# A tile of their own for the extra tokens' values, and a second room for the last chunk's probabilities

## The chip, the cores and the metric

The kernel runs on one core of one Trainium2 chip. Time is the device time of one execution in microseconds (us). The kernel before took 1063.71 us (median of 3 runs, 1061.87 to 1066.89). One further execution was profiled; it took 1059.23 us.

## What is computed

One layer of a hybrid decoder. A prompt of 2048 tokens (16 chunks of 128) and 48 extra tokens (8 sequences of 4 decode tokens, and 16 meta tokens) are layer-normed and projected by one input matrix. Half of the width goes through an mLSTM, evaluated chunk by chunk with a carried state; the other half through sliding-window attention (window 128, meta tokens visible to all, one learned sink per head). Both are gated, projected and merged with the residual:

```python
def mlstm_chunk(state, q, k, v, log_i, log_f):
    ...
    qk = jnp.einsum('bthd,bshd->btsh', q, k) * w
    num = jnp.einsum('btsh,bshd->bthd', qk, v) + jnp.einsum('bthk,bhkv->bthv', q, c) * s_inter[..., None]
    ...
    c_new = decay[..., None, None] * c + jnp.einsum('bsh,bshk,bshv->bhkv', w_state, k, v)
...
    s = jnp.einsum('bnqkgd,bnskd->bnkgqs', qb, kcat)
    s = jnp.where(mask[None, :, None, None], s, -jnp.inf)
    o_real = jnp.einsum('bnkgqs,bnskd->bnqkgd', sink_softmax(s, sink), vcat)
...
    mix = jnp.concatenate([y_m, y_a], axis=-1).astype(w_o.dtype) @ w_o
    return layer_norm(DN_ALPHA * x + mix.astype(x.dtype), g, b)
```

## The kernel before

All large products run as three f16 products of split numbers (high and low halves). A projection of one chunk by one 512-wide weight is therefore 24 matmuls of 128x512 (`proj`, lines 296 to 301), summed in one PSUM tile `pj`. There are two such tiles, and a projection can only start when one has been read out by VectorE.

**Phase A** (to about 550 us) takes the 16 chunks through the mLSTM. `a_steps(n)` projects queries, keys, values and output gate (`a_proj(n, 0..3)`, the weights `w_q`, `w_k`, `w_v`, `w_o`), reads each out (L430 for the values, L433 for the others), and does the recurrence: gates (`a_gate`, L513 and L516), running sums (`m_rows`, L749 to L759), weights (`m_weights`, L768 to L787), scores (`m_S`, L803), outputs (`m_num`, L816 and L817), state (`m_kv`, L832). Between these steps `jobs()` is advanced: first the decode tokens' recurrence (`d_prepare`, `d_head`), later the other weights' preparation. Before the loop the extra tokens are projected by the same four weights (`proj_e`, L307 and L308); the results `qe`, `ke`, `ve`, `oe` are written to DRAM as `e_d`, and each `d_head(h)` reads its head from there into `eh` (in the tile `da`), which its first matmul, the transpose L699, needs. `kwe` and `ve` also make the meta tokens' state (L651).

A chunk's values lie in `vaug[n % 2]`, two tiles of 4 heads by 129 columns whose last column is one. The extra tokens' values `ve` are put into `vaug[1]`, which is also the tile of chunk 1.

**Phase B** runs the attention, the gates and the output projection chunk by chunk. `s_unit(n, u)` treats two heads: scores (L1271), masked maximum (L1272), exponentials (L1278), and the split of the probabilities into `hl` (high half by ScalarE, L1279; low half by VectorE, L1280). After every second unit one DMA transpose takes `hl` to `pT`, which `s_pv` (L1324) multiplies with the values. There is one `hl` tile, so unit 2 of a chunk may write it only when the transpose of units 0 and 1 has read it.

Tiles come from pools by tag: a tile of a tag with one buffer can be written when the one before it has been read for the last time. The tag `wkv` has one buffer, which holds in turn the layer-norm rows `gbr`, the arenas of the extra tokens (`e_arena`, 2048 words a partition, handed out piece by piece by `take`) and, in phase B, the key and value weights.

The order of the instructions on each engine is not the order of the code. A scheduler sets it at build time from its own estimate of when each instruction can run. On the chip each engine then goes through its list strictly in order, and an instruction whose input is late holds everything behind it. SyncE (SP) issues all the DMAs, in order as well.

Of the kernel before, what the change touches and what calls it, by code (L numbers as in the profile page):

```python
# [9 lines left out]
F16 = mybir.dt.float16  # L10
# [6 lines left out]
P = 128  # L17
D = 1024
KT = 8
NCH = 16  # L20
NM = 16
NS = 32
NE = NS + NM
H = 4
# [17 lines left out]
def tile_hymba_step(  # L42
# [7 lines left out]
    V, A, G, T, S = nc.vector, nc.scalar, nc.gpsimd, nc.tensor, nc.sync  # L50
# [4 lines left out]
    mn = ctx.enter_context(tc.tile_pool(name="mn", bufs=1))  # L55
# [9 lines left out]
    def pt(shape):  # L65
        return psum("pt", shape, 3)
# [14 lines left out]
    def work(tag, shape, dt=F32, bufs=None):  # L81
        return mn.tile(shape, dt, tag=tag, name=tag, bufs=bufs or KB4.get(tag, 1))
# [23 lines left out]
    def dmat(out, in_):  # L106
        return dma(out, in_, S.dma_start_transpose)
# [108 lines left out]
    vaug = [cst.tile([P, H, 129], F32, name=f"vaug{i}") for i in range(2)]  # L216
# [319 lines left out]
    def e_arena():  # L536
        return Arena(mn.tile([P, 2048], F32, tag="wkv", name="ea"))

    E = St()
    ea = e_arena()  # L540
# [2 lines left out]
    qe = work("qs", [P, 512])[:NE]  # L543
    ke = work("At", [P, 512])[:NE]
    oe = work("g", [P, 512])[:NE]
    ve = vaug[1][:NE]

    sto = stage(512, "w")
    load(sto, w_a[3])
# [9 lines left out]
    hl = work("hl", [P, 2, D], F16)  # L559
    ln0_(xe, NE, hl.rearrange("p c d -> p (c d)").bitcast(BF16)[:NE])  # L560
    split_e(EE[:, 0], xe, NE, s_x)
    dmat(ET, EE[:, 0])
    xef = ea.take(8 * NE).rearrange("p (k t) -> p k t", t=NE)
    ps = pt([P, 8, NE])
    for j in range(8):
        T.transpose(ps[:, j], xe[:, j * P:(j + 1) * P], ident[:NE, :NE])
# [80 lines left out]
    for j in range(2):  # L647
        ps = po([P, 2, 256])
        for i in range(2):
            h = 2 * j + i  # L650
# [605 lines left out]
    def s_unit(n, u):  # L1256

        c = cb[n]
        pvc = cb.get(n - 1)
        lo = 0 if pvc is not None else P  # L1260
        if u % 2 == 0:
            c.hl = work("hl", [P, 2, 4, 256], F16)
        hl, q, h0 = c.hl, u % 2, 2 * u
        mxs, nb, sums = c.mxs, c.nb, c.sums
        mask = swamask[:, c.half, lo:]
        p = work(("g", "SI")[u % 2], [P, 2, NW])
        for i in range(2):
            h = h0 + i
            ps = pt([P, NW])
            for x in range(2):  # L1270
                T.matmul(ps[:, lo:], c.qT[:, h], kTs[:, 2 * (h // 4) + x, lo:], start=(x == 0), stop=(x == 1))  # L1271
            V.tensor_tensor_reduce(p[:, i, lo:], ps[:, lo:], mask, sc_s, sink60[:, h:h + 1],  # L1272
                                   op0=ALU.add, op1=ALU.max, accum_out=mxs[:, h:h + 1])
        hs = slice(h0, h0 + 2)
        V.tensor_scalar(nb[:, hs], mxs[:, hs], -1.0, LN2x12, op0=ALU.mult, op1=ALU.add)  # L1275
        for i in range(2):
            h = h0 + i
            A.activation(p[:, i, lo:], p[:, i, lo:], AF.Exp, bias=nb[:, h:h + 1], accum_out=sums[:, h:h + 1])  # L1278
        A.activation(hl[:, 0, 2 * q:2 * q + 2, lo:], p[:, :, lo:2 * P], AF.Copy)  # L1279
        V.tensor_tensor(hl[:, 1, 2 * q:2 * q + 2, lo:], p[:, :, lo:2 * P], hl[:, 0, 2 * q:2 * q + 2, lo:],  # L1280
                        op=ALU.subtract)
        m = c.mhl[:, u // 2, :, 2 * q:2 * q + 2]
        A.activation(m[:, 0], p[:, :, 2 * P:], AF.Copy)  # L1283
        G.tensor_tensor(m[:, 1], p[:, :, 2 * P:], m[:, 0], op=ALU.subtract)  # L1284
        if lo:
            G.memset(hl[:, :, 2 * q:2 * q + 2, 0:P], 0.0)
        if q:
            pT = work("stg", [P, 2, 4, 2, P], F16)
            dmat(out=pT.rearrange("p c h e q -> p (c h e) q"),
                                  in_=hl.rearrange("p c h k -> p (c h k)"))  # L1290
            c.PT.append(pT)
# [88 lines left out]
    for n in range(NCH - 1):  # L1380
        b_load(n + 1)
        b_q(n)
        b_kv(n)
        if n > 0:
            s_pv(n - 1)
        b_az(n)
        if n == 2:
            b_out(0)
        s_start(n)
        s_unit(n, 0)  # L1390
        s_unit(n, 1)
        b_z(n)
        s_unit(n, 2)
        s_unit(n, 3)
        s_sums(n)
        if n == 0:
            z = work("xs", [P, D])[:NS]
            dma(z, ze_d)
            final(z, NS, y_s)
        elif 1 < n < NCH - 2:  # L1400
            b_out(n - 1)
            cb.pop(n - 2, None)

    n = NCH - 1
# [113 lines left out]
```

## Time and profile before

| | |
|---|---|
| time, median of 3 runs | 1063.71 us (1061.87 to 1066.89) |
| profiled execution | 1059.23 us, of which 1057.4 us are the span from the first to the last instruction |
| TensorE busy with matmuls (PE) | 1026.1 us |
| VectorE (DVE) busy | 728.7 us |
| ScalarE (ACT) busy | 441.3 us |
| GpSimd (POOL) busy | 247.6 us |

In a row of the timeline stand: start in us, length in us, engine, line, operation, output<-inputs by the program's names, output<-input (partitions x elements, type), count. In brackets stands how long the engine was idle just before, and what ended that. In a row of the waits view: the waiting instruction, what it waited for, us in total, times, longest. In a row of the windows view: the stretch and its length, then for each engine the busy time (and the number of instructions), the clock granted to TensorE as a share of full, the busy share of the DMA engines, and GB/s. SPq is SyncE's queue, which issues DMAs.

### The profile page before, as it was taken

How to read it: one execution, taken by the hardware profiler on the slowest of the kernel's cores; microseconds unless marked ns; L12 is line 12 of the kernel's file. 1: busy time of each engine (PE TensorE's matmuls, PEld its weight loads, DVE VectorE, ACT ScalarE, POOL GpSimd, SP SyncE). 2: the span in 40 equal slices, each digit the busy share in tenths (PEclk: the TensorE clock that was granted, in tenths of full speed). 3: DMA queues.
4: the chain of work that ended last, by engine and by line, in shares of the span. 5: the costliest groups of instructions: out<-in, count | busy, mean ns of one | idle time of the engine just before them, and what ended most of it. 6: DMA issues, size and time to landing. Idle time of an engine off the chain costs nothing.

```text
span 1057.4 us, 17650 instructions
## 1 busy us (share of the span) xinstructions
PE 1026.1 (97%) x6399; PEld 571.0 (54%) x6399; DVE 728.7 (69%) x2056; ACT 441.3 (42%) x1112; POOL 247.6 (23%) x270
## 2 busy tenths in 40 slices
PE   7998999999999999999999999999999999999996
PEld 3544666655556555555565555555555455555552
DVE  5996876767766887787557676656566566666674
ACT  5783333336244554552334334343334333343430
POOL 2101313211111001013111332233331233332322
PEclk9998999999999999999999999999999999999998
DMA  9946366464794775755866463555445555545452
GB/s 332 267 133 164 99 145 154 115 187 88 233 236 123 222 247 140 231 133 160 291 188 124 92 160 89 132 131 117 108 113 127 128 124 139 108 102 135 113 114 76
DMA packets 245809, 161.83 MB, mean 153 GB/s; under 512 B 207945, under 2 KB 220953, under 8 KB 244409
## 3 DMA queue, kind: packets, MB, share of 16 engines
q1 hardware_dynamic: 245722, 160.70, 58.3%
q8 instruction: 50, 0.82, 0.3%
q14 instruction: 37, 0.30, 0.1%
HBM read 68.22 MB, written 43.58 MB: 106 GB/s over the span
## 4 chain that ended last, share of the span: by engine, by line
PE 69%; DMA 11%; DVE 10%; ACT 6%; issue 3%; POOL 1%; SPq 1%; DVEq 0%; ACTq 0%
PE pj L1351 14%; PE pj L301 14%; PE pj L298 14%; PE pj L299 14%; DMA stg<-hl 3%; PE pt L1271 3%; PE po L1324 2%; DMA stg<-in_dram 1%; DMA xT<-hl 1%; DMA kT<-kh 1%; ACT w_o L259 1%; DMA wd_o<-w_o 1%; DVE w_o L276 1%; PE po L816 1%; PE po L817 1%
## 5 line engine op out<-in xcount | busy, mean ns | idle before, releaser
L301 PEld LDWEIGHTS <-xT 128*128 128x128 f16 x992 | 96.9, 98 | 98.2 <-issue 1.0
L299 PEld LDWEIGHTS <-xT 128*128 128x128 f16 x992 | 97.4, 98 | 96.7 <-issue 5.2
L298 PEld LDWEIGHTS <-xT 128*128 128x128 f16 x992 | 97.4, 98 | 94.1 <-issue 2.8
L1351 PEld LDWEIGHTS <-EE 128*128 128x128 f16 x720 | 70.3, 98 | 79.0
L1351 PE MATMUL pj<-wr_o,EE 128*128 128x512 f16 x360 | 82.3, 379 | 0.0
L1351 PE MATMUL pj<-w_o,EE 128*128 128x512 f16 x360 | 82.1, 379 | 0.0
L1278 ACT ACTIVATE SI<-SI,nb 128x272 f32<-128x272 f32 (+1 forms) x64 | 32.4, 507 | 66.0 <-DVE nb L1275 66.0
L298 PE MATMUL pj<-w_o,xT 128*128 128x512 f16 x120 | 46.9, 390 | 3.2 <-DVE vaug L430 3.2
L1278 ACT ACTIVATE g<-g,nb 128x272 f32<-128x272 f32 (+1 forms) x64 | 32.2, 503 | 42.4 <-DVE nb L1275 42.4
L1284 POOL TENSOR_TENSOR mhl<-SI,mhl 128x32 f16<-128x32 f32 x32 | 12.6, 395 | 157.6 <-ACT mhl L1283 157.6
L298 PE MATMUL pj<-wr_az,xT 128*128 128x512 f16 x128 | 48.5, 379 | 0.0
L299 PE MATMUL pj<-wr_z,xT 128*128 128x512 f16 x128 | 48.5, 379 | 0.0
L298 PE MATMUL pj<-wr_aq,xT 128*128 128x512 f16 x128 | 48.5, 379 | 0.0
L299 PE MATMUL pj<-wr_aq,xT 128*128 128x512 f16 x128 | 48.5, 379 | 0.0
L299 PE MATMUL pj<-wr_az,xT 128*128 128x512 f16 x128 | 48.5, 379 | 0.0
L298 PE MATMUL pj<-wr_z,xT 128*128 128x512 f16 x128 | 48.5, 379 | 0.0
L793 POOL TENSOR_TENSOR qs<-qs,SI 128x512 f32<-128x512 f32 x16 | 20.9, 1307 | 113.5 <-ACT SI L784 113.3
L299 PE MATMUL pj<-w_o,xT 128*128 128x512 f16 x120 | 46.7, 390 | 0.0
L1181 POOL TENSOR_TENSOR xs<-xs,gb 128x1024 f32<-128x1024 f32 (+1 forms) x16 | 42.8, 2674 | 15.4 <-DMA stg<-hl 9.3
L298 PE MATMUL pj<-w_v,xT 128*128 128x512 f16 x120 | 46.0, 383 | 0.0
L299 PE MATMUL pj<-w_v,xT 128*128 128x512 f16 x120 | 45.8, 382 | 0.0
L792 POOL TENSOR_TENSOR qs<-qT 128x512 f32<-128x512 f16 x16 | 20.2, 1260 | 109.2 <-DMA qT<-qh 58.9
(463 smaller groups left out, 2492.1 us busy)
## 6 DMA issues: line engine op xcount, KB each, us to landing
stg<-in_dram SPq DMA_DIRECT2D x28, 512.0 KB
xs<-in_dram SPq DMA_DIRECT2D x16, 512.0 KB
h_d<-xs SPq DMA_DIRECT2D x16, 512.0 KB
xT_d<-xT SPq DMA_DIRECT2D x16, 512.0 KB
xs<-h_d SPq DMA_DIRECT2D x16, 512.0 KB
xT<-xT_d SPq DMA_DIRECT2D x16, 512.0 KB
out_dram<-xs SPq DMA_DIRECT2D x15, 512.0 KB
hn_d<-g SPq DMA_DIRECT2D x16, 258.0 KB
```

The lines of the kernel that those rows point to most:

```text
L259: A.activation(w.t[:, 2 * i:2 * i + 2, 0, :], s, AF.Abs, accum_out=mx4[:, i:i + 1])
L298: T.matmul(ps, xT[:, k, :], w.t[:, k, 0, :n], start=(k == 0), stop=False)
L299: T.matmul(ps, xT[:, k, :], w.t[:, k, 1, :n], start=False, stop=False)
L301: T.matmul(ps, xT[:, KT + k, :], w.t[:, k, 0, :n], start=False, stop=(k == KT - 1))
L792: G.tensor_tensor(c.qs, c.qT[:, 0], c.qT[:, 1], op=ALU.add)
L793: G.tensor_tensor(c.qs, c.qs, c.SI, op=ALU.mult)
L1181: G.tensor_tensor(z, z, lg[:rows], op=ALU.mult)
L1271: T.matmul(ps[:, lo:], c.qT[:, h], kTs[:, 2 * (h // 4) + x, lo:], start=(x == 0), stop=(x == 1))
L1278: A.activation(p[:, i, lo:], p[:, i, lo:], AF.Exp, bias=nb[:, h:h + 1], accum_out=sums[:, h:h + 1])
L1284: G.tensor_tensor(m[:, 1], p[:, :, 2 * P:], m[:, 0], op=ALU.subtract)
L1324: T.matmul(pso[:, h], l, r, start=False, stop=(i == len(last) - 1), skip_group_check=True)
L1351: T.matmul(ps, c.yT[:, a, :], w[:, k, t, :], start=(first and j == 0), stop=(last and j == len(mm) - 1))
```

## The change

```diff
@@ -543,7 +543,8 @@
     qe = work("qs", [P, 512])[:NE]
     ke = work("At", [P, 512])[:NE]
     oe = work("g", [P, 512])[:NE]
-    ve = vaug[1][:NE]
+    ve = ea.take(H * 129).rearrange("p (h d) -> p h d", d=129)[:NE]
+    G.memset(ve[:, :, 128:129], 1.0)
 
@@ -560,7 +561,7 @@
-    xef = ea.take(8 * NE).rearrange("p (k t) -> p k t", t=NE)
+    xef = work("kw", [P, 512])[:, 0:8 * NE].rearrange("p (k t) -> p k t", t=NE)
@@ -1259,7 +1260,10 @@
         if u % 2 == 0:
-            c.hl = work("hl", [P, 2, 4, 256], F16)
+            if n == NCH - 1 and u == 2:
+                c.hl = mn.tile([P, 2, 4, 256], F16, tag="wkv", name="hl2")
+            else:
+                c.hl = work("hl", [P, 2, 4, 256], F16)
```

The extra tokens' values move from `vaug[1]` into the arena `ea`, with a memset of their own for the column of ones. The transposed extra tokens `xef`, which lay in the arena, move to the tile of the tag `kw`, which makes the room. In the last chunk, units 2 and 3 write their probabilities into a tile `hl2` in the room of the key and value weights, whose last matmul is that chunk's own projection.

No instruction is removed, and one memset is added; but the scheduler's order changes with it. On TensorE it differs from the extra tokens' projection by `w_o` to the end of phase A, and is the same after that; on the other engines it also differs in the last chunk. Line numbers of the changed kernel are higher by 1 from L547 on, and by 4 from L1267 on.

On VectorE, where chunk 1's values are read out of PSUM (L430), before. `mx` are the maxima over the staged weights of the next job, `stg`; `g` at L311 and L317 is the extra tokens' output gate:

```order
L759 SCALAR_TENSOR_TENSOR rM<-r_712,cols,rb 128x128
L696 COPY da<-ea 128x8
L614 COPY ea<-pt 48x12
L644 TENSOR_SCALAR kw<-At,ea 48x128 x4
L696 COPY da<-ea 128x8
L261 TENSOR_REDUCE mx_1803<-stg 128x1 x2
L311 TENSOR_TENSOR g<-g,bias 48x512
L261 TENSOR_REDUCE mx_1803<-stg 128x1
L317 SCALAR_TENSOR_TENSOR g<-px,cols,g 48x512
L430 SCALAR_TENSOR_TENSOR vaug_125<-pj,cols,bias 128x4x128
```

The same place of the changed kernel, where L317 in the first row writes `ve`:

```order
L317 SCALAR_TENSOR_TENSOR ea<-px,cols,g 48x4x128
L759 SCALAR_TENSOR_TENSOR r_714<-fi,cols,rb 128x128
L430 SCALAR_TENSOR_TENSOR vaug_125<-pj,cols,bias 128x4x128
L760 SCALAR_TENSOR_TENSOR rM<-r_714,cols,rb 128x128
L697 COPY da<-ea 128x8
L615 COPY ea<-pt 48x12
L697 COPY da<-ea 128x8
L645 TENSOR_SCALAR kw<-At,ea 48x128 x4
L261 TENSOR_REDUCE mx_1805<-stg 128x1 x2
L311 TENSOR_TENSOR g<-g,bias 48x512
```

L430 has moved ahead of the reads of `stg` and ahead of the two copies into `da`.

On TensorE behind the extra tokens' projection by `w_o`, before. The 12 matmuls L803 are followed by the 16 gate matmuls L513 and L516, then by chunk 1's 24 matmuls by `w_o`, and then by L699:

```order
L308 MATMUL px<-w_o,EE 128x512
L768 MATMUL pt<-rM,sel 128x128 x4
L651 MATMUL po<-vaug_125,kw 128x129 x4
L771 MATMUL pt<-cs,r_712 128x128 x2
L665 MATMUL pt<-ea,sel 128x40 x4
L803 LDWEIGHTS kT
L803 MATMUL pt<-qT,kT 128x128
```

In the changed kernel 8 of chunk 1's matmuls by `w_o` stand ahead of these small ones; the piece begins with the last of the 8:

```order
L299 MATMUL pj<-w_o,xT 128x512
L769 MATMUL pt<-rM,sel 128x128
L652 MATMUL po<-ea,kw 128x129 x4
L769 MATMUL pt<-rM,sel 128x128 x3
L772 MATMUL pt<-cs,r_714 128x128 x2
L666 MATMUL pt<-ea,sel 128x40 x4
L298 LDWEIGHTS xT
L298 MATMUL pj<-w_o,xT 128x512
```

Then come 13 more by `w_o` (14 in all behind the small ones), 10 of the 12 L804, and this, still on TensorE:

```order
L804 MATMUL pt<-qT,kT 128x128
L700 MATMUL px<-cs,da 128x32 x2
L804 LDWEIGHTS kT
L804 MATMUL pt<-qT,kT 128x128
L804 LDWEIGHTS kT
L804 MATMUL pt<-qT,kT 128x128
L513 LDWEIGHTS xT
L513 MATMUL pt<-w_g,xT 128x16
```

L700, the transpose that was L699, now stands ahead of 2 of the L804, of the gates and of the last 2 matmuls by `w_o`; before, it stood behind all of them. On SyncE the load `da<-e_d`, which it needs, has moved ahead of the transpose of the chunk's queries. Before:

```order
L104 DMA stg<-in_dram 128x512 x3
L104 DMA e_d<-vaug_125 48x4x128
L104 DMA stg<-in_dram 128x512
L104 DMA e_d<-g 48x512
L104 DMA_TRANSPOSE qT<-qh 128x8x128
L104 DMA da<-e_d 32x4x128
```

And of the changed kernel:

```order
L104 DMA stg<-in_dram 128x512 x3
L104 DMA e_d<-ea 48x4x128
L104 DMA stg<-in_dram 128x512
L104 DMA e_d<-g 48x512
L104 DMA da<-e_d 32x4x128
L104 DMA_TRANSPOSE qT<-qh 128x8x128
```

The two loads of `stg` and the two writes to `e_d` keep their places; only the last two rows have changed sides.

On ScalarE in the last chunk, before. `SI` holds units 1 and 3, `g` unit 2; L994 and L1326 belong to the gates and to the chunk before:

```order
L1279 ACTIVATE hl<-SI 128x512
L1283 ACTIVATE mhl<-SI 128x32
L1283 ACTIVATE mhl<-g 128x32
L994 ACTIVATE kw<-kT 128x512
L1278 ACTIVATE SI,sums<-SI,nb 128x272 x2
L1300 ACTIVATE es<-es 128x8
L1283 ACTIVATE mhl<-SI 128x32
L1279 ACTIVATE hl<-g 128x512
L1279 ACTIVATE hl<-SI 128x512
```

And of the changed kernel:

```order
L1283 ACTIVATE hl<-SI 128x512
L1287 ACTIVATE mhl<-SI 128x32
L1283 ACTIVATE hl_11037<-g 128x512
L1287 ACTIVATE mhl<-g 128x32
L995 ACTIVATE kw<-kT 128x512
L1282 ACTIVATE SI,sums<-SI,nb 128x272 x2
L1304 ACTIVATE es<-es 128x8
L1283 ACTIVATE hl_11037<-SI 128x512
L1287 ACTIVATE mhl<-SI 128x32
```

Unit 2's copy into `hl2` now follows unit 1's at once, and unit 3's stands ahead of its small piece `mhl`. VectorE's halves (L1284) have moved with them: unit 2's now stands ahead of the read-out `kT` (L1228). On SyncE the transpose of `hl2` stands behind that of `mhl`, as before, but now ahead of the load of the residual `xs<-h_d`.

## The prediction

> **What bounds the kernel now.** The page comes first, then the waits of TensorE in total.
>
> ```profile
> span 1057.4 us, 17650 instructions
> PE 1026.1 (97%) x6399; PEld 571.0 (54%) x6399; DVE 728.7 (69%) x2056; ACT 441.3 (42%) x1112; POOL 247.6 (23%) x270
> PE po L1324 <- DMA stg<-hl: 5.1, 5, 2.1
> PE pj L298 <- DVE vaug L430: 3.2, 1, 3.2
> PE pt L749 <- DVE Gf L483: 2.9, 2, 1.7
> ```
>
> TensorE is busy for 1026.1 of 1057.4 us, the next engine for 728.7. So time can only be won where TensorE stands still, about 31 us in all; and what delays another engine costs only if TensorE then stands still longer. The part that the change can touch is this list of waits. Two of them are its subject: the wait of a projection for L430 (3.2 us), and the longest of the waits for the probabilities' transposes (2.1 us).
>
> The first wait, in the timeline:
>
> ```profile
> 78.77 0.38 PE L301 MATMUL pj<-w_v,xT 128*128 128x512 f16 x1
> 84.20 1.05 PE L768 MATMUL pt<-rM,sel 128*128 128x128 f32 x8
> 87.36 0.84 PE L803 MATMUL pt<-qT,kT 128*128 128x128 f16 x12
> 88.03 0.35 PE L513 MATMUL pt<-w_g,xT 128*128 128x16 f16 x8
> 88.24 0.34 PE L516 MATMUL pt<-w_g,xT 128*128 128x8 f16 x8
> 91.77 0.58 PE L298 MATMUL pj<-w_o,xT 128*128 128x512 f16 x1 [3.19 <-DVE vaug L430]
> 99.23 0.31 PE L699 MATMUL px<-cs,da 32*128 32x32 f32 x2
> 99.47 0.39 PE L298 MATMUL pj<-w_q,xT 128*128 128x512 f16 x1
> 80.62 0.33 DVE L758 SCALAR_TENSOR_TENSOR r<-fi,cols,rb 128x128 f32<-128x128 f32 x1
> 85.54 0.17 DVE L696 COPY da<-ea 128x8 f32<-128x8 f32 x1 [1.53 <-DMA da<-in_dram]
> 87.72 1.50 DVE L261 TENSOR_REDUCE mx<-stg 128x1 f32<-128x512 f32 x2 [2.00 <-DMA stg<-in_dram]
> 90.33 0.73 DVE L317 SCALAR_TENSOR_TENSOR g<-px,cols,g 48x512 f32<-48x512 f32 x1
> 90.99 0.73 DVE L430 SCALAR_TENSOR_TENSOR vaug<-pj,cols,bias 128x512 f32<-128x512 f32 x1
> 91.09 0.34 SPq L104 DMA_DIRECT2D e_d<-g  x1
> 93.16 0.68 SPq L104 DMA_DIRECT2D da<-e_d  x1
> 96.45 0.31 ACT L706 ACTIVATE da<-da 32x128 f32<-32x128 f32 x1 [1.23 <-DMA da<-e_d]
> ```
>
> VectorE waits 2.00 us for a staged weight at L261, and L430 stands behind that, so chunk 1's projection by `w_o` starts at 91.77. It then runs slowly, as the windows view shows (cut where the granted clock changes; it stands behind the five busy times, ahead of the DMA share; two other places with waits stand below):
>
> ```profile
> 85.99:89.40 3.41, 2.59 (x42) 2.40 (x41) 1.56 (x3) 1.68 (x6) 0.00 (x0) 1.00 0.85 285
> 89.40:96.23 6.83, 4.46 (x11) 1.57 (x11) 5.92 (x21) 2.77 (x8) 1.27 (x1) 0.50 0.44 67
> 96.23:99.64 3.41, 3.41 (x17) 1.49 (x16) 3.19 (x7) 1.31 (x5) 1.89 (x1) 1.00 0.00 0
> 393.19:396.60 3.41, 1.58 (x26) 0.98 (x24) 1.48 (x7) 3.39 (x8) 0.00 (x0) 1.00 0.55 155
> 396.60:400.01 3.41, 3.41 (x10) 1.18 (x9) 3.31 (x8) 3.41 (x11) 1.54 (x1) 0.50 0.30 111
> 1031.48:1034.90 3.42, 1.57 (x28) 1.11 (x29) 2.71 (x4) 0.10 (x1) 0.00 (x0) 1.00 0.79 165
> 1034.90:1038.30 3.40, 3.40 (x17) 1.57 (x16) 0.72 (x2) 0.63 (x1) 0.00 (x0) 1.00 0.24 48
> ```
>
> The clock was at 0.50 from 89.40 to 96.23. Of that, TensorE worked from 91.77 on, 4.46 us at half speed, which lost 2.2 us. The place costs 3.2 + 2.2 = 5.4 us.
>
> **The change, part by part.** *The place at 90 us.* L430 now stands ahead of L261, behind L758 (80.62). Its PSUM tile is complete with the last matmul by `w_v` (78.77) and nothing holds `vaug[1]` any more, so it runs at about 81 us, and `w_o` finds its tile free. From 84.20 on TensorE has, by the rows above: 8 matmuls by `w_o` (0.21 us each, by two that follow each other, 491.46 and 491.67 below) 1.7 us; the small ones L768 to L665, which took from 84.20 to 87.36, 3.2 us; 14 more by `w_o`, 3.0 us; 10 of the 12 L803, which took 0.67 us, 0.6 us. It reaches L700, once L699, at 92.7 us. L652, now behind the 8, needs `kw` from L645, which now stands behind the copy that waited for its transfer until 85.54; TensorE comes at 86.2, and the first quarter of `kw` is there by then.
>
> L700 reads `da<-e_d`. That load waits for `e_d<-g`, and this for L317 (90.33), which stands behind L261 and its wait as before. Neither has moved: `e_d<-g` is issued at 91.09, and the load, which waits for its landing, at 93.16. Before, the load landed at 96.45, when ScalarE got it; TensorE came at 99.23 and did not notice. Now TensorE comes 6 us earlier and stands still. **The wait is exchanged, not removed.** How long? Ahead of the load there was a transpose on SyncE's queue, which now stands behind it. The nearest row is the write `e_d<-g`, done 93.16 - 91.09 = 2.1 us after its issue; the slow end is the 3.3 us of before. I take 2.1: the load lands at 95.3, a wait of 2.6 us. After that come L700 (0.24, from 99.23 to 99.47), 2 L804 (0.1), the gates (0.4) and 2 by `w_o` (0.4): `w_q` starts at 96.4 instead of 99.47, with the same work done. That is 3.1 us, at full clock; with the slow end 1.9. What queues behind this wait: on VectorE L724 waits for the same load and holds the read-out of `k`, whose PSUM tile `w_q` needs; a read-out takes 0.73 us (L430), L724 is a small one (32x128), and TensorE's own work ahead of `w_q` takes 1.1, so it adds nothing. On SyncE the queries' transpose comes 2 us later; the scores that need it stand behind chunk 2's queries and keys.
>
> The clock is the second half. Of the 3.41 us behind 92.7, TensorE would work some 0.8 us (23%), less than in the stretch at 393.19 (1.58 us, 46%), behind which the clock fell to 0.50 for one such stretch. Against it speaks the stretch at 1031.48, as idle (1.57 us), behind which it stayed at 1.00. I take one stretch at half clock, 1.7 us. The place then gives 3.1 - 1.7 = 1.4 us; with two stretches and the slow load it costs 1.5 us; with no wait at all it gives 5.4.
>
> The Trainium skill ("TensorE: Matmul & The Clock Gate", section "Part 1: The HAM clock gate (the "warmup" mystery)") says that the clock falls to half after at least one idle window of about 3.4 us. By that rule a wait of 2.6 us would leave the clock at full, and the place would give 3.1 us. The stretch at 393.19, with 1.58 us of work in it and half clock behind it, speaks against the rule.
>
> *The memset of `ve`'s ones, `xef` in another tile.* A memset of 48x4 on GpSimd, busy 247.6 of 1057 us, ahead of anything TensorE waits for: nothing. The tile of `kw` is next written by `kwe` (L645), a projection and more behind the last reader of `xef`: nothing.
>
> *The rest of phase A.* The order is shuffled to its end, with the same work. The larger waits there, L749 2.9 us above and L513 1.8 us below, and the half clock behind L513 (1.7 us), are 6.4 us in all. They may vanish or come twice. One can be followed:
>
> ```profile
> 491.46 0.38 PE L298 MATMUL pj<-w_o,xT 128*128 128x512 f16 x1
> 491.67 0.38 PE L299 MATMUL pj<-w_o,xT 128*128 128x512 f16 x1
> 493.76 0.30 PE L749 MATMUL pt<-cs,Gf 128*128 128x128 f32 x1 [1.71 <-DVE Gf L483]
> 395.29 0.34 PE L513 MATMUL pt<-w_g,xT 128*128 128x16 f16 x8 [1.83 <-ACT am L773]
> ```
>
> Ahead of the L749 of the last chunk now stand 9 matmuls of the projection instead of 4: 5 x 0.21 = 1.1 us of cover, if VectorE's gates come as before. I count 1.1 us (from 0 to 1.7). At 395 us TensorE waits for L773, which stands behind four L259 on ScalarE; in the new order L773 stands further back, but so does L513, and the copy `fi`, which the next weights need, has come behind the first L259. A wait goes and one comes: nothing, between 3.5 us won (this wait and its half clock) and 3.5 lost.
>
> *The last chunk.*
>
> ```profile
> 1018.46 2.32 DVE L1280 TENSOR_TENSOR hl<-SI,hl 128x512 f16<-128x512 f32 x1 [0.43 <-ACT hl L1279]
> 1017.51 2.73 POOL L1181 TENSOR_TENSOR xs<-xs,gb 128x1024 f32<-128x1024 f32 x1 [0.93 <-DVE xs L1180]
> 1025.15 0.19 ACT L1300 ACTIVATE es<-es 128x8 f32<-128x8 f32 x1
> 1025.46 0.63 ACT L1279 ACTIVATE hl<-g 128x512 f16<-128x512 f32 x1
> 1025.85 1.18 SPq L104 DMA_TRANSPOSE mT<-mhl  x1
> 1027.12 0.53 SPq L104 DMA_DIRECT2D xs<-h_d  x1
> 1028.08 3.17 SPq L104 DMA_TRANSPOSE stg<-hl  x1
> 1033.33 0.87 PE L1324 MATMUL po<-vd,stg 128*128 128x64 f16 x24 [2.14 <-DMA stg<-hl]
> ```
>
> Unit 2's copy (1025.46) has no idle time ahead of it: ScalarE did not wait for the transpose of `hl` at that point, the scheduler had only put it late. With `hl2` it runs directly behind unit 1's, and unit 3's copy directly behind L1300. But unit 2's low half (0.6 us) now stands on VectorE ahead of unit 3's read-outs and delays them, and `mhl`, now behind unit 3's copy, comes 0.6 us later, so `mT` is issued at about 1027. It holds SyncE for 1.2 us, so the transpose of `hl2` starts at about 1028.2, not before 1028.08. What is won is that the load `xs<-h_d` no longer runs ahead of it: the transpose took 5.2 us to land (1028.08 to 1033.33). I count 0.5 us, between 2.1 (the whole wait) and -1.7: L1280 at 1018.46 took 2.32 us while GpSimd's L1181 ran, instead of about 0.7, and unit 2's low half could meet L1182 in the same way.
>
> *Sum:* 1.4 + 0 + 1.1 + 0.5 = 3.0 us. Against the profiled execution's own 1059.23 us: 1056.2. The median of the runs shown is 4.5 us above that execution, so the time forecast is 1063.7 - 3.0 = **1060.7 us**.
>
> **The rivals.** (a) *The wait at L700 leaves the clock at full*, as behind 1031.48: 1.7 us more, 1059.0. (b) *No wait at L700*: the load lands when TensorE comes. For it: SyncE reaches the load directly behind the write. Against it: VectorE's wait for `stg` at 87.72 is a wait for a transfer, and it has not moved. The place then gives 5.4, and 7.0 with the other terms: 1056.7. (c) *Nothing comes of it*: unit 2's copy did not wait, so the second part does nothing, and the shuffled order gives back the rest: 1063.7. (d) *Slower*: the load `da<-e_d` lands late. From 96.6 on, with one stretch at half clock, the place gives nothing (99.47 - 96.6 - 1.1 - 1.7), and each further us costs one; from 98.2 on the 1.6 us of the other terms are eaten up as well. With a landing at 99 and two stretches at half clock (3.4 us) the place costs 4.1 us, and with the other terms the time is 1066.2. For it: in the windows about 89 us the DMA engines moved up to 285 GB/s, and a load then took 3.3 us. Against it: at 96 us they moved nothing.
>
> **How the numbers follow.** Forecast 0.43, (a) 0.21, (b) 0.14, (c) 0.12, (d) 0.10. The range holds eight in ten: 1055.0, from (b) with the wait at 493.76 gone entirely (0.6) and 1.1 more of the last wait, to 1066.5, from (d). 0.5% is 5.3 us, about what a measurement of this kernel tells from no change. Faster by more than that is (b) almost whole and some of (a) and of the forecast where the shuffled stretch also gains: 0.25. Slower by more is half of (d) and a shuffle that loses twice its waits: 0.07. Within it: 0.68.
>
> **What would show it.** The wait for L430 is gone and L430 starts near 81; the waits of TensorE name L700 and `da<-e_d` with 2 to 4 us; the granted clock is half for one stretch of 3.4 us behind it; the first `w_q` starts near 96.4 plus what the clock loses. The last chunk's L1328 (once L1324) waits 1 to 2 us. No L700 in the list of waits would make (b) right; waits of several us between 100 and 500 us would make the forecast wrong where it counted nothing.

## The result and the profile after

The changed kernel takes 1069.51 us (median of 8 runs, 1068.98 to 1072.62); the kernel before took 1062.62 us beside it (8 runs, 1060.57 to 1066.89). The ratio is 1.0055, with an interval of 1.0039 to 1.0071: slower, by about 5.9 us by the ratio (the two medians lie 6.9 us apart). The forecast was 1060.7 us, and the range ended at 1066.5.

The page of the changed kernel and TensorE's waits in total:

```profile
span 1067.3 us, 17652 instructions
PE 1027.5 (96%) x6399; PEld 570.6 (53%) x6399; DVE 734.9 (69%) x2056; ACT 442.2 (41%) x1112; POOL 248.9 (23%) x271
...
PE po L1328 <- DMA stg<-hl: 4.9, 6, 1.7
PE pt L804 <- DMA kT<-kh: 3.9, 1, 3.9
PE px L700 <- DMA da<-e_d: 2.9, 1, 2.9
PE pt L769 <- DVE rM L760: 2.5, 2, 2.3
PE pt L750 <- DVE g L819: 2.2, 1, 2.2
```

TensorE's busy time has hardly grown (by 1.4 us); it stands still longer. The wait for L430 is gone, the wait at L700 has come in its place, and around it stand waits that the list of before didn't have. Three places show what happened.

**At 90 us** (the timeline):

```profile
80.40 0.73 DVE L430 SCALAR_TENSOR_TENSOR vaug<-pj,cols,bias 128x512 f32<-128x512 f32 x1
87.53 1.31 DVE L261 TENSOR_REDUCE mx<-stg 128x1 f32<-128x512 f32 x2 [1.55 <-DMA stg<-in_dram]
89.95 0.73 DVE L317 SCALAR_TENSOR_TENSOR g<-px,cols,g 48x512 f32<-48x512 f32 x1
90.71 0.34 SPq L104 DMA_DIRECT2D e_d<-g  x1
92.71 0.67 SPq L104 DMA_DIRECT2D da<-e_d  x1
95.31 0.28 PE L700 MATMUL px<-cs,da 32*128 32x32 f32 x2 [2.91 <-DMA da<-e_d]
96.90 0.63 PE L298 MATMUL pj<-w_q,xT 128*128 128x512 f16 x1
```

L430 runs at 80.40. The load `da<-e_d` still hangs on L317, and that on L261's wait for the weights, so TensorE stands at L700 for 2.91 us. Chunk 2's first projection starts at 96.90 instead of 99.47, 2.6 us earlier. The windows show the clock at this place, at the next one, and the sums of phase A from chunk 2 on:

```profile
92.24:95.65 3.41, 0.50 (x8) 0.33 (x6) 2.15 (x13) 2.93 (x11) 0.09 (x1) 1.00 0.07 19
95.65:99.06 3.41, 3.41 (x26) 1.48 (x25) 3.28 (x4) 1.19 (x5) 3.41 (x2) 0.50 0.65 82
...
266.40:269.80 3.40, 3.40 (x33) 2.28 (x32) 3.40 (x5) 1.29 (x3) 1.37 (x1) 0.51 1.05 443
...
97.00:572.00 475.00, 461.06 (x2867) 267.40 (x2866) 341.78 (x981) 192.62 (x450) 85.22 (x79) 0.99 0.63 173
```

The same sum for the kernel before:

```profile
99.50:564.00 464.50, 458.35 (x2868) 267.63 (x2868) 335.60 (x979) 191.75 (x450) 82.17 (x77) 1.00 0.64 176
```

Both stretches run from chunk 2's first projection to the first read-out of phase B's keys and hold the same matmuls (one record is missing in one of them). TensorE stands still for 475.00 - 461.06 = 13.9 us in it, before for 6.2: **7.8 us of new waits, and 2.7 us of longer work**. About 1 us of the longer work is half clock: 2.1 us of one stretch and the 3.41 us of another here, one stretch of 3.41 us before (396.60 to 400.02).

**At 266 us** lies the largest new wait (the timeline of the changed kernel):

```profile
248.85 0.73 DVE L433 SCALAR_TENSOR_TENSOR k<-pj,cols,bias 128x512 f32<-128x512 f32 x1
255.78 1.06 ACT L323 ACTIVATE hl<-xs 128x1024 bf16<-128x1024 f32 x1 [9.14 <-DMA xT<-hl]
256.83 0.71 ACT L437 ACTIVATE kh<-k,cols 128x512 f16<-128x512 f32 x1
257.57 0.91 DVE L438 SCALAR_TENSOR_TENSOR kh<-k,cols,kh 128x512 f16<-128x512 f32 x1 [6.95 <-ACT kh L437]
258.82 2.25 SPq L104 DMA_TRANSPOSE kT<-kh  x1
266.26 1.44 PE L804 MATMUL pt<-qT,kT 128*128 128x128 f16 x12 [3.89 <-DMA kT<-kh]
```

The keys `k` of chunk 6 are read out at 248.85, but their split L437 stands on ScalarE behind L323, which waits 9.14 us for the tile `hl` of another chunk. The same place before:

```profile
250.48 0.74 DVE L433 SCALAR_TENSOR_TENSOR k<-pj,cols,bias 128x512 f32<-128x512 f32 x1
261.48 1.28 SPq L104 DMA_TRANSPOSE kT<-kh  x1
267.90 0.83 PE L803 MATMUL pt<-qT,kT 128*128 128x128 f16 x12
```

There the transpose was issued even later, 11.0 us behind the read-out instead of 10.0, and nobody waited: TensorE had other matmuls until 267.90, 17.4 us behind the read-out. In the new order it has them for 13.5 us only (266.26 - 3.89 - 248.85). The way from the read-out to the landed transpose takes 17.4 us in the new order, which the old one's cover would just have hidden. The cover has shrunk: between the last matmul by `w_k` and the scores the trace has 111 matmuls before and 84 in the new order, where the next chunk's projection by `w_q` no longer stands among them. Behind the wait comes half clock, 0.51 in the window from 266.40 on.

**At 397 us**, the place that the prediction put at nothing:

```profile
394.12 1.06 ACT L259 ACTIVATE w_o<-stg 128x1024 f16<-128x1024 f32 x1 [4.46 <-DMA wd_z<-w_z]
395.29 0.39 ACT L753 ACTIVATE fi<-pt 128x256 f32<-128x256 f32 x1
395.50 0.68 DVE L1036 TENSOR_TENSOR ea<-ea 32x512 f32<-32x512 f32 x1 [4.46 <-DMA ea<-hne_d]
397.44 0.82 PE L769 MATMUL pt<-rM,sel 128*128 128x128 f32 x5 [2.32 <-DVE rM L760]
```

The wait for L773 went, and one for `rM` came, behind two instructions that each wait 4.46 us for a transfer.

In the spans the account is: -2.6 us to chunk 2, +10.6 to phase B (572.2 - 96.90 against 564.2 - 99.47), +3.0 in phase B, -1.1 in the last chunk, together 9.9. That is more than the medians say (6.9), because the profiled execution of before lay 3.4 us under the median of its runs. The first and the last read-out of phase B's keys, before:

```profile
L1227 DVE SCALAR_TENSOR_TENSOR kT<-pj,cols,bias x8: 716/750/752, 564.2 to 1020.7; 128x512 f32<-128x512 f32 x8
```

and of the changed kernel:

```profile
L1228 DVE SCALAR_TENSOR_TENSOR kT<-pj,cols,bias x8: 718/750/751, 572.2 to 1031.7; 128x512 f32<-128x512 f32 x8
```

The last read-out is a late mark in the changed kernel, since unit 2's low half now stands ahead of it on VectorE: it runs 1.84 us behind TensorE's first matmul by `wr_z` of the last chunk, before 1.18. Counted from that matmul (1019.53 before, 1029.87 after), phase B grew by 2.3 us, and the last chunk shrank by 0.4.

### The profile page after: what moved, and what is told of

It is laid out like the page before. It is cut to its first block, busy times and chain, and to the rows that moved or that the text cites. A ratio compares the mean times of both kernels' runs of the same rounds, so it can differ in the third digit from the quotient of the medians.

```text
span 1067.3 us, 17652 instructions
## 1 busy us (share of the span) xinstructions
PE 1027.5 (96%) x6399; PEld 570.6 (53%) x6399; DVE 734.9 (69%) x2056; ACT 442.2 (41%) x1112; POOL 248.9 (23%) x271
## 4 chain that ended last, share of the span: by engine, by line
PE 55%; DMA 17%; DVE 13%; ACT 6%; SPq 4%; issue 4%; POOL 1%; DVEq 0%; ACTq 0%; POOLq 0%
PE pj L1355 13%; PE pj L301 11%; PE pj L298 10%; PE pj L299 10%; SPq L104 4%; DMA stg<-hl 3%; PE pt L1275 2%; DMA xT<-hl 2%; DMA stg<-in_dram 2%; PE po L1328 2%; ACT w_o L259 1%; DMA wd_z<-w_z 1%; DMA wt<-hn_d 1%; DVE w_o L276 1%; DMA wd_o<-w_o 1%
## 5 line engine op out<-in xcount | busy, mean ns | idle before, releaser
L327 POOL TENSOR_TENSOR lns<-lns,mhalf 128x1 f32<-128x1 f32 (+1 forms) x16 | 19.0, 1186 | 141.9 <-ACT lns L326 115.2
L793 POOL TENSOR_TENSOR qs<-qT 128x512 f32<-128x512 f16 x16 | 19.4, 1211 | 128.8 <-DMA qT<-qh 84.0
L298 PE MATMUL pj<-w_q,xT 128*128 128x512 f16 x120 | 46.7, 389 | 0.0
L299 PE MATMUL pj<-w_q,xT 128*128 128x512 f16 x120 | 46.5, 388 | 0.0
L1182 POOL TENSOR_TENSOR xs<-xs,gb 128x1024 f32<-128x1024 f32 (+1 forms) x16 | 42.8, 2675 | 15.2 <-DVE xs L1181 7.4
L298 PE MATMUL pj<-w_o,xT 128*128 128x512 f16 x120 | 45.5, 379 | 0.5 <-DVE k L433 0.5
L298 PE MATMUL pj<-w_k,xT 128*128 128x512 f16 x120 | 45.5, 379 | 0.0
```

Of the source, the lines that this page charges most:

```text
L298: T.matmul(ps, xT[:, k, :], w.t[:, k, 0, :n], start=(k == 0), stop=False)
L299: T.matmul(ps, xT[:, k, :], w.t[:, k, 1, :n], start=False, stop=False)
L327: G.tensor_tensor(rs, ve, mhalf[:rows, 0:1], op=ALU.pow)
L793: G.tensor_tensor(c.qs, c.qT[:, 0], c.qT[:, 1], op=ALU.add)
L1182: G.tensor_tensor(z, z, lg[:rows], op=ALU.mult)
```

## The experiments

Two theories stand against each other. **The order**: the changed tiles cost nothing, and the new order that the scheduler makes from them loses the time. **The tiles**: the new places of `ve` and `xef`, the memset, or the second room cost time by themselves, whatever the order. Each ratio below is to the kernel before, run beside the kernel.

### One part at a time

`p1_values` has the first two pieces of the diff alone, `p2_room` the last piece alone.

> The first part alone (ve in the arena, xef in kw's room; one hl as before). Its order in phase A is that of the changed kernel, instruction by instruction. Theory (the loss is new waits in phase A's new order): as slow as the whole change or 0.5 us slower, 1069 to 1071 us, ratio to before 1.006, with the waits of 4 us for kT<-kh near 266 us and of 2.3 us for rM near 397 us in the trace. Rival (the loss comes from the second room for the probabilities or from the attention phase): back at before's 1062.6 us or below it.

> The second part alone (hl2 in the room of wkv; ve in vaug[1] as before). Its order in phase A is before's. Theory: 0 to 1 us faster than before, 1061.6 to 1062.6 us, no wait for kT<-kh near 266 us, the last long wait for stg<-hl 0.3 to 0.6 us shorter. Rival (the second part is what costs): 1066 to 1069 us.

`p1_values`: 1071.43 us, 1.0073 (1.0047 to 1.0099). `p2_room`: 1062.12 us, 0.9985 (0.9967 to 1.0002). The first part carries the whole loss, and with it comes the new order of phase A; the second part leaves that order as it was, and costs nothing.

### Mending the new waits

If the order loses the time, taking out its largest waits should win it back. `m1_kh_first` puts chunk 6's key split ahead of L323 on ScalarE, by an edge that the scheduler must keep:

```diff
+        if n == 8:
+            with tc.issue_after(ca[n - 2].hi):
+                ln0_(xs, P, hl.rearrange("p c d -> p (c d)").bitcast(BF16))
...
-                A.activation(hl[:, 0], t, AF.Copy, scale=s_qk[i])
+                c.hi = A.activation(hl[:, 0], t, AF.Copy, scale=s_qk[i]).ins
```

`m123_two_sites` adds two such edges at 397 us: `fi` ahead of the four L259, and `rM` ahead of L1036.

```diff
+                with tc.issue_after(w.fi):
+                    A.activation(w.t[:, 2 * i:2 * i + 2, 0, :], s, AF.Abs, accum_out=mx4[:, i:i + 1])
...
+        with tc.issue_after(carry.M):
+            V.tensor_tensor(E.z[:NS], E.z[:NS], E.t1[:NS], op=ALU.mult)
```

> The changed kernel with one order edge on ScalarE: chunk 6's copy of the keys' high half (kh, L437) is issued ahead of chunk 8's layer-norm sum (hl, L323), which waits for a DMA transpose to have read hl. Theory (that misplaced copy makes the keys 7 us late): the wait of 3.9 us for kT<-kh and the half clock behind it (1.7 us) go, 1063.9 us, at least 4 us less than the changed kernel, ratio to before 1.001 (0.999 to 1.003). Rival (the transposes are late for SyncE's queue and the DMA traffic of the staged weights at 257 us): the wait stays above 2 us, 1067 to 1069.5 us. Second rival (the time lost is lost in any case, something else is late by as much): 1069 us with another wait near 266 us.

> As m1_kh_first, and at 397 us two more edges: the copy of the gate rows (fi, L753) ahead of the four L259 on ScalarE, which wait for the write of w_z to DRAM, and the running sums L757 to L760 ahead of the product L1036 on VectorE, which waits for a load. Theory: another 2.3 us, the wait for rM at 397 us, goes: 1061.6 us, 2 us below m1_kh_first, ratio to before 0.999 (0.997 to 1.001). Rival (the wait moves to the next late thing at that place, the queries' transpose or L774): no different from m1_kh_first.

`m1_kh_first`: 1067.88 us, 1.0056 (1.0032 to 1.0080). `m123_two_sites`: 1068.37 us, 1.0037 (1.0016 to 1.0058). 1063.9 and 1061.6 us were forecast; little or nothing came back, and the intervals tell neither run from the changed kernel. The timeline of `m1_kh_first` at 266 us:

```profile
251.15 0.74 DVE L442 SCALAR_TENSOR_TENSOR kh<-k,cols,kh 128x512 f16<-128x512 f32 x1
...
258.27 1.23 SPq L104 DMA_TRANSPOSE kT<-kh  x1
...
264.63 0.84 PE L808 MATMUL pt<-qT,kT 128*128 128x128 f16 x12 [1.60 <-DMA kT<-kh]
```

`kh` is complete 6 us earlier, yet its transpose is issued at 258.27, since on SyncE's queue other transfers stand ahead of it. A wait of 3.89 us has become one of 1.60. `m4_keys_ahead` therefore moves the transpose as well (in the changed kernel's own order, held fixed; how is shown below):

```diff
 L104 DMA_TRANSPOSE qT<-qh
+L104 DMA_TRANSPOSE kT<-kh
 L104 DMA xT_d_141<-xT
 L104 DMA hn_d_171<-g
 L104 DMA stg<-in_dram x3
-L104 DMA_TRANSPOSE kT<-kh
```

> The changed kernel with its own order pinned and two rows moved: chunk 6's copy kh (L437) ahead of L323 on ScalarE, as in m1_kh_first, and on SyncE its transpose kT<-kh directly behind qT<-qh, ahead of the write xT_d (which waits until xT has landed), hn_d and three staged weights. Theory Q (after m1 the keys were late for SyncE's queue): the transpose is issued near 254 us instead of 258.3, lands before TensorE comes at 262.2, and no wait and no half clock are left at 262 us; at most the two small waits at 272 us (1.7 us) stay: 1065 us, ratio to before 1.002 (1.000 to 1.004). Rival D (the transfers themselves are slow there, with the DMA engines busy for 1.0 of the time): the transpose lands 7 us after its issue again and more than 1 us of wait stays: 1067 us.

1068.61 us, 1.0040 (1.0018 to 1.0061), where 1065 us was forecast. The timeline:

```profile
253.56 2.45 SPq L104 DMA_TRANSPOSE kT<-kh  x1
263.11 0.83 PE L804 MATMUL pt<-qT,kT 128*128 128x128 f16 x12
270.58 0.73 DVE L433 SCALAR_TENSOR_TENSOR o<-pj,cols,bias 128x512 f32<-128x512 f32 x1
271.36 0.38 PE L298 MATMUL pj<-w_k,xT 128*128 128x512 f16 x1 [1.38 <-DVE o L433]
```

The scores now wait for nothing, and 8 us later the next projection waits 1.38 us for a read-out that stands late in VectorE's list. Behind a late transfer stood a late queue, and behind that a late read-out: a wait that is taken out shows the next one. That the new waits are what the new order costs rests on the sums of phase A above; these three runs don't show it, since none of them won back more than the intervals leave open.

### Other orders of both kernels

If it is the order, another order of the changed kernel need not lose, and another order of the kernel before may. `pace(.92)` says how fast the other jobs are drawn into the loop; a slightly different number makes the scheduler mix them otherwise, in both kernels, with the same work.

```diff
-            if pace(.92):
+            if pace(.91):
```

`a_` is the changed kernel and `b_` the one before, with .91 and .93.

> The changed kernel with another order of phase A: the side jobs are advanced in 91 of 100 steps instead of 92; same tiles, same work. Theory O (the loss is the luck of one order: which waits a reshuffled list happens to have): anywhere from 1060 to 1072 us, with waits at other places than 266 and 397 us, and no steady distance to before's tiles at the same rate. Theory S (once chunk 1's values need not wait, TensorE runs ahead into a stretch where transfers limit, and loses there whatever the order): 1067 to 1071 us, 5 to 7 us above before's tiles at the same rate.

> The kernel before (ve in vaug[1]) with the side jobs advanced in 91 of 100 steps. Theory O: another order, so another time, from 1060 to 1072 us. Theory S: as before, 1061 to 1065 us, since the wait at 90 us that keeps TensorE back is still there.

> The changed kernel with the side jobs advanced in 93 of 100 steps. Theory O: from 1060 to 1072 us, not bound to the value at 91. Theory S: 1067 to 1071 us, 5 to 7 us above before's tiles at 93.

> The kernel before with the side jobs advanced in 93 of 100 steps. Theory O: from 1060 to 1072 us. Theory S: 1061 to 1065 us.

| | .91 | .92 | .93 |
|---|---|---|---|
| changed | 1.0064 (1.0039 to 1.0090) | 1.0055 (1.0039 to 1.0071) | 1.0019 (1.0004 to 1.0034) |
| before | 1.0068 (1.0049 to 1.0087) | 1 | 1.0055 (1.0037 to 1.0073) |

The two kernels have no steady gap: they are level at .91, and the changed one is the faster at .93. The waits also change with the order. The largest of `b_rate93`, a kernel without the change, behind the one at the kernel's start:

```profile
PE pt L749 <- DVE Gf L483: 4.2, 1, 4.2
```

What stands out is the kernel before with .92: its order is better than the other five in the table, by 0.2 to 0.7%.

### The changed tiles in the old order

`r1_old_order` is the whole changed kernel, but the list of each engine is held to that of `p2_room`, which in phase A is that of the kernel before. The function adds order edges alone; it takes no wait away:

```diff
+def pin(tc, nc):
...
+    for e, runs in PIN.items():
+        ins = by[getattr(mybir.EngineType, e)]
+        last = None
+        for r in runs.split():
+            a, _, m = r.partition(":")
+            for i in ins[int(a):int(a) + int(m or 1)]:
+                if last is not None:
+                    tc.add_manual_dep(i, last.name, info, reason="pin")
+                last = i
```

> The whole changed kernel (same tiles, same memset), but with every engine's list pinned to the order that the scheduler made for p2_room, which in phase A is before's order. Chunk 1's values no longer have to wait, but L430 still stands behind the reads of stg. Theory (the time lost is the new order, not the tiles): as p2_room, 1061 us, ratio to before 0.9985 (0.996 to 1.001). Rival (the tiles, the memset or the place of xef cost): 1066 us or more.

1064.56 us, 1.0004 (0.9986 to 1.0022). **The tiles cost nothing that shows; the order was the loss.** By the interval the tiles could cost up to 2.3 us of the 5.9. (The opposite, the old tiles in the new order, was not run.) The wait for L430 is back in full, as before the change:

```profile
PE pt L750 <- DVE Gf L483: 4.6, 2, 3.4
...
PE pj L298 <- DVE vaug L430: 3.0, 1, 3.0
```

Now the change can be used alone. `r2_one_row` moves one row of VectorE's list, L430, which the new tile of `ve` allows; `r3_three_rows` also moves the extra tokens' gate ahead of the reads of `stg`:

```diff
 L760 SCALAR_TENSOR_TENSOR rM<-r_714,cols,rb 128x128
+L430 SCALAR_TENSOR_TENSOR vaug_125<-pj,cols,bias 128x4x128
 L697 COPY da<-ea 128x8
...
-L261 TENSOR_REDUCE mx_1805<-stg 128x1 x2
 L311 TENSOR_TENSOR g<-g,bias 48x512
-L261 TENSOR_REDUCE mx_1805<-stg 128x1
 L317 SCALAR_TENSOR_TENSOR g<-px,cols,g 48x512
-L430 SCALAR_TENSOR_TENSOR vaug_125<-pj,cols,bias 128x4x128
-L261 TENSOR_REDUCE mx_1805<-stg 128x1
+L261 TENSOR_REDUCE mx_1805<-stg 128x1 x4
```

(the row L430 is `r2_one_row`, all rows are `r3_three_rows`).

> As r1_old_order with one row moved: on VectorE, chunk 1's read-out L430 stands directly behind L760, ahead of the copies into da and the reads of stg. This is the first part of the change without the reshuffle. Theory: the wait of 3.2 us for L430 goes, a wait of 2 to 3.5 us for da<-e_d comes at L700, and w_q starts some 2.6 us earlier, as in the changed kernel; what is won there stays: 1058.5 us, 1 to 3 us below r1_old_order, ratio to before 0.996 (0.994 to 0.998). Rival (TensorE, once ahead, loses it again at 160 and 266 us as the changed kernel did): as r1_old_order, with new waits there.

> As r2_one_row, and on VectorE the extra tokens' gate (L311, L317) also ahead of the reads of stg, so that e_d is written and read back some 4 us earlier. Theory: no wait at L700, no half clock at 90 us; the place gives its whole 5.4 us: 1056 us, 2 to 3 us below r2_one_row. Rival (the load of da lands late for the transfers around it): a wait at L700 of more than 1 us is left, 1058 us.

`r2_one_row`: 1061.11 us, 0.9977 (0.9955 to 0.9999), 2.9 us better than `r1_old_order` by the two ratios, with an uncertainty of as much. Its timeline and windows:

```profile
96.62 0.28 PE L700 MATMUL px<-cs,da 32*128 32x32 f32 x2 [2.49 <-DMA da<-e_d]
96.83 0.39 PE L298 MATMUL pj<-w_q,xT 128*128 128x512 f16 x1
...
92.32:95.74 3.42, 1.81 (x9) 0.61 (x7) 2.95 (x16) 2.78 (x8) 1.15 (x1) 1.00 0.57 121
95.74:99.15 3.41, 2.53 (x13) 1.29 (x14) 2.64 (x4) 1.22 (x4) 2.01 (x2) 1.00 0.86 157
```

This is the first part of the change with TensorE's and SyncE's lists as before: a wait of 2.5 us at L700, and `w_q` at 96.83 instead of 99.47. Unlike in the changed kernel, the clock stays at full behind the wait. `r3_three_rows`: 1061.85 us, 0.9970 (0.9949 to 0.9991), where 2 to 3 us less than `r2_one_row` was forecast. Its timeline:

```profile
94.24 0.31 PE L700 MATMUL px<-cs,da 32*128 32x32 f32 x2
94.48 0.39 PE L298 MATMUL pj<-w_q,xT 128*128 128x512 f16 x1
...
101.55 0.33 PE L750 MATMUL pt<-cs,Gf 128*128 128x128 f32 x1 [1.57 <-DVE Gf L483]
```

With `g` early there is no wait at L700, and `w_q` starts 2.3 us earlier still; but 7 us behind it TensorE waits 1.57 us for the gates, and between the two ratios lies nothing that the intervals tell apart.

### More rows

`r4_four_places` adds three moves to `r3_three_rows`: L145 behind L483 on VectorE (317 us), L774 ahead of the four L259 on ScalarE (396 us), and the two products L1182 and L1183 behind the next L793 and L794 on GpSimd (495 us). `r5_six_rows` has the first two of them, and instead of the third it moves TensorE's L750 and L751 back, behind 8 more matmuls by `w_q` at 102 us and behind 10 more by `w_o` at 494 us:

```diff
-L145 TENSOR_REDUCE rmx<-rm 128x1
 L480 SCALAR_TENSOR_TENSOR ls<-ls 128x4 x4
...
 L483 SCALAR_TENSOR_TENSOR Gf_120<-ls 128x4
+L145 TENSOR_REDUCE rmx<-rm 128x1
...
+L774 ACTIVATE am<-pt 128x8
 L259 ACTIVATE w_o_4145,mx_4146<-stg 128x2x512 x4
-L774 ACTIVATE am<-pt 128x8
...
-L750 MATMUL pt<-cs,Gf_121 128x128
-L751 MATMUL pt<-cs,Gi_123 128x128
 L298 MATMUL pj<-w_q,xT 128x512
...
+L750 MATMUL pt<-cs,Gf_121 128x128
+L751 MATMUL pt<-cs,Gi_123 128x128
```

> As r3_three_rows, and one row moved at each of three later places where TensorE waits in p2_room: at 317 us the maximum L145, which waits for a load, behind the gates' L483 on VectorE (wait 1.2); at 396 us the copy L774 ahead of the four L259 on ScalarE, which wait for the write of w_z (wait 2.6, and half clock); at 495 us GpSimd's products L1182 and L1183 behind the next L793 and L794, since VectorE's small operations of the gates took 1.6 to 2.2 us beside them (wait 3.5). Theory: 5 to 8 us less than r3_three_rows, 1049 us (1047 to 1052), ratio to before 0.987. Rival (each place has a next late thing close behind): 1 to 3 us less.

> As r3_three_rows, and four more moves: L145 behind L483 at 317 us and L774 ahead of L259 at 396 us as in r4_four_places; at 102 us the transposes L750 and L751 behind the next 8 matmuls of w_q, and at 494 us behind the next 10 of w_o, so that TensorE has work while VectorE finishes the gates. GpSimd's L1182 and L1183 stay where they were. Theory: 1.6 us at 102, 1.4 at 317, 0 to 1.5 at 396 and 2 us at 494 are won, and rM, which was ready 2.7 us and more ahead of its matmul at both places, holds nothing: 1056 us, 4 to 7 us below r3_three_rows, ratio to before 0.992 (0.990 to 0.994). Rival (as in r4, what is won comes back at the next late thing): within 2 us of r3_three_rows.

`r4_four_places`: 1060.81 us, 0.9973 (0.9953 to 0.9994), no better than `r3_three_rows`, where 5 to 8 us were forecast. The wait at 495 us is gone from its list and has come back at 520 us:

```profile
519.09 0.49 DVE L1167 TENSOR_SCALAR bias<-bias,cols 128x512 f32<-128x512 f32 x1 [8.35 <-DMA bias<-in_dram]
519.90 0.79 PE L833 MATMUL po<-vaug,kw 128*128 128x129 f32 x2 [4.64 <-DVE Cst L834]
```

The two products feed a write on SyncE's queue, which was issued at 505.56 instead of 494.06 in `r3_three_rows`. The transfers behind it now stand close together, and the transpose of the queries held the queue for 5.41 us instead of 2.71. So the load of `bias` was issued at 516.86, hardly ahead of the 517.79 of `r3_three_rows`, although VectorE was 7.0 us further on (it read out the keys at 510.00 instead of 517.01). VectorE waits 8.35 us for that load, ahead of the state L834 that TensorE needs.

`r5_six_rows`: **1058.14 us, 0.9936 (0.9915 to 0.9957)**: faster than both kernels. Its timeline at the two places where TensorE's rows moved:

```profile
93.28 0.39 PE L298 MATMUL pj<-w_q,xT 128*128 128x512 f16 x1
100.20 0.27 PE L750 MATMUL pt<-cs,Gf 128*128 128x128 f32 x1
...
484.99 2.21 DVE L478 TENSOR_SCALAR ls<-ls 128x4 f32<-128x4 f32 x1
484.81 2.35 POOL L1183 TENSOR_TENSOR xs<-xs,gb 32x1024 f32<-32x1024 f32 x1
490.56 0.77 PE L833 MATMUL po<-vaug,kw 128*128 128x129 f32 x2 [3.09 <-DVE g L819]
```

At 100 us the wait of `r3_three_rows` is gone. At 490 us the move didn't help: L833, the next matmul that needs VectorE, waits 3.09 us for the same late engine. How the 6.8 us divide over the moves isn't known; only the place at 90 us was timed by itself. Against `r3_three_rows` the ratio is 3.6 us better, a little less than the 4 to 7 forecast.

## Why the prediction was wrong, point by point

**The place at 90 us** was right in mechanism and nearly in size. L430 was put at 81 us (it ran at 80.40), the load's landing at 95.3 (L700 ran at 95.31), the wait at 2.6 us (2.91), then one stretch at half clock (0.50 from 95.65 to 99.06). The wait was exchanged, as forecast: `w_q` came 2.6 us earlier, and the half clock behind 96.90 took back about 1.1, so the gain is 1.5 us where 1.4 was forecast. `r2_one_row`, which moves L430 alone, measured 2.9 us, with an uncertainty of as much. Rival (b), no wait at L700, was wrong for the reason given: L261's wait had not moved. `r3_three_rows` showed what it takes, `g` ahead of L261.

**The clock** at that place followed the forecast, and not rival (a): of the 3.41 us behind 92.24 TensorE worked 0.50, and half clock came, as in the four other runs with this order of phase A at the place (`p1_values`, `m1_kh_first`, `m123_two_sites`, `m4_keys_ahead`). That part is not a property of the wait alone: in `r2_one_row` a wait of 2.49 us for the same load left the clock at full, as rival (a) had it. Which of the two comes goes by how the wait falls on the clock's steps (last section), and no row of the trace before told that: the right call was in part luck. The rule of the Trainium skill ("TensorE: Matmul & The Clock Gate", section "Part 1: The HAM clock gate (the "warmup" mystery)"), that it takes an idle window of about 3.4 us, doesn't hold here: the wait was 2.91 us.

**The memset and `xef` at nothing** was right: `r1_old_order` has them all and stands at 1.0004.

**The last chunk** was right in size. The tail of the changed kernel:

```profile
1043.19 0.87 PE L1328 MATMUL po<-vd,stg 128*128 128x64 f16 x24 [1.67 <-DMA stg<-hl]
```

The wait is 1.67 us where it was 2.14: 0.5 us, as counted, and by the way forecast: the transpose of `hl2`, issued at 1038.84, is used 4.35 us later, that of `hl` before 5.25 us after its issue. In the twelve kernels with the second room this wait is 1.6 to 1.7 us, in the four without it 1.8 to 2.4. `p2_room` measured 0.9985, with an interval that holds both this and nothing.

**"The rest of phase A" is the step that failed.** It held that the shuffled order has "the same work", that the old waits "may vanish or come twice", and it counted +1.1 us. The spans show 10.6 us lost from chunk 2 to phase B (with about 1.1 of them from the half clock at 90 us). By the ratios the changed kernel stands 5.4 us above `r1_old_order`, although its order includes the gain at 90 us, of 1.5 us (2.6 less the clock) to 2.9; so the rest lost some 7 to 8. Three things were wrong in the step.

- It bounded the new waits by the old ones. The places that stood still before (L749, L513) were followed, and those that stood covered were not. The largest new wait is at one of the latter: chunk 6's keys at 266 us, with 17.4 us of cover before and 13.5 after. That could have been seen: the number of matmuls between the keys' last and the scores, 84 instead of 111, stood in the new order.
- The one place it did count, the L749 of the last chunk with 1.1 us of cover won, went the other way: L750 waits 2.2 us there for VectorE instead of 1.71. Even with an unchanged list that wait isn't fixed: it was 1.7 us before, and 3.4 in `r1_old_order`.
- It took the old order for a typical one, so that gain and loss were equally likely. It was a good one: the five others that the scheduler made of the two kernels, the changed kernel's own among them, were all slower, by 0.2 to 0.7%, four of them by 0.55% or more. That the old order was so good was luck, and only runs of other orders could tell. A shuffle away from an order that is better than its neighbours loses on average, and the chance of 0.07 for slower was far too small.

Rival (d), slower, had the wrong mechanism: the load landed on time. The slower time came from no single place, but from eight waits of 0.5 to 3.9 us between 160 and 503 us, with half clock behind the largest; before there were four in that stretch, of 0.6 to 1.8 us.

Open: phase B took 2.3 us longer than before in the profile of the changed kernel (3.0 by its first and last read-out of keys), though its list is the same up to the last chunk. TensorE waits 1.6 us in it for the load `kTs<-kd`, for which it didn't wait before; but `p2_room` and `r1_old_order`, with the old order, wait 1.1 us for it too. The times between its first and last read-out of keys lie between 455.5 and 459.9 us over the sixteen kernels profiled, and the five with the changed kernel's order, or that with one to three edges or two rows moved, at the upper end (458.5 to 459.9); `r2_one_row` and `r4_four_places`, with the old order and a few rows moved, have 459.7 and 458.6. It was not followed further. And one profile is only one draw: three of the old order (before, `p2_room`, `r1_old_order`) reach phase B at 564.2, 566.2 and 571.0 us, two of the new (the changed kernel, `p1_values`) at 572.2 and 573.8.

## What to carry to other kernels

Where a scheduler sets the order, every change of a tile or a dependency is also a new draw of the order, and its spread (here 0.2 to 0.7%) can be larger than what the change is meant to give: measure a few other orders first, and test the change itself with the order held fixed. To forecast a new order, don't ask only what becomes of the waits that are there: count for each transferred operand the matmuls between its producer and its user, before and after; at 266 us a wait came where that cover shrank below the transfer's time. On engines that go through a list in order, move what TensorE waits for ahead of an instruction that waits for a transfer, one row at a time, and look at once for the wait that stands next.

## What the runs showed of the hardware

- **Half clock comes after short stands, and where they fall decides.** Over the sixteen traces, from 60 us on, a stand is the start of a matmul later than usual (the shortest distance for its form) behind the one before it. Behind 57 stands of 1.25 to 2.0 us the clock in the next 5 us was lowered 4 times; behind 29 of 2.0 to 3.0 us, 19 times; behind 17 of 3.0 us or more, 15 times. Within each trace all changes of the clock lie on one grid of 3.41 us (before: 89.41, 96.23, 396.60 and 400.02, which are 2, 88 and 1 steps apart). Between 60 and 1048 us, every step of that grid at full clock in which TensorE worked less than 1.5 us was followed by a step at half clock (30 of 30); of those with 1.5 to 1.9 us of work, 4 of 30; of the 4505 others, 5. In the changed kernel the wait at L700 lies in one step (0.50 us of work); in `r2_one_row` it is divided between two (1.81 and 2.53 us), and the clock stayed. In all, 34 of the 46 stands above 2 us had the clock lowered, and a step at half clock costs up to 1.7 us.
- **Some of VectorE's small operations stretch beside GpSimd's products.** L478 on 128x4 took 2.21 us beside L1183 in `r5_six_rows` (its median there is 0.17 us), more than a read-out of 128x512 takes by itself (0.73 us), and both ended at 487.2. L476 took 1.60 us and ended with L1182 at 484.7; L475, which also ran beside L1182, kept to 0.15 us. The chain of gates is made of such operations, and at about 494 us TensorE waited for it or for what stands behind it before the change, behind it and in `r5_six_rows`.
- **An early operand doesn't make an early transfer.** In `m1_kh_first` the transpose of `kh` was issued 7.1 us after its last writer L442 had started, because SyncE's queue held other transfers ahead of it; in `r4_four_places` the queue stood 17.6 us for the product L1183 ahead of a write, and the load of `bias` behind that write was issued 6.9 us after VectorE's read-out of the keys, in `r3_three_rows` 0.8 us.
